# Finished sums of a feed-forward product stay in their PSUM banks instead of going to the stream one by one

## The chip, the cores and the metric

The kernel runs on one core of a Trainium2 chip. The metric is the device time of one execution in microseconds (us); lower is better. Runs of the kernel before: 1672.14, 1674.78 and 1675.12 us, median 1674.78.

## The reference

Two decoder layers over one sequence of 512 tokens with 1024 features, all float32:

```python
for l in range(DEPTH):                                   # DEPTH = 2
    x = x + 0.5 * swiglu(rms_norm(x, ffn1_norm[l]), ffn1_wg[l], ffn1_wu[l], ffn1_wd[l])
    h = rms_norm(x, mix_norm[l])
    z = h @ w_in[l]                                      # q | k | v | conv_B | conv_C | conv_h
    ...                                                  # windowed attention, short convolution
    x = x + jnp.concatenate([attn_out, conv_out], axis=-1) @ w_out[l]
    x = x + 0.5 * swiglu(rms_norm(x, ffn2_norm[l]), ffn2_wg[l], ffn2_wu[l], ffn2_wd[l])
return rms_norm(x, final_norm)

def swiglu(h, w_gate, w_up, w_down):                     # 1024 -> 2816 -> 1024
    return (jax.nn.silu(h @ w_gate) * (h @ w_up)) @ w_down
```

The change touches the last product of the four `swiglu` calls, `... @ w_down`, and its addition to `x`.

## The kernel before, in words

**Precision.** Every float32 operand is split in two: a high part `hi` (a cast on ScalarE, L205) and a remainder `lo = raw - hi` (a subtraction on VectorE, L206). A product is three TensorE passes: hi by hi, hi by lo, lo by hi. Weight pieces are 128x1024; their parts live in `wh` and `wl`, three buffers each, filled in the order written down by `plan` and taken by `take_split`, which keeps two pieces ahead. A buffer of `wh` is free again when TensorE has used the piece three before.

**The stream.** `x` stays in SBUF as eight tiles `xt(t, o)`, 128 tokens `t` by 512 features `o`.

**One feed-forward part** (`ffn`) goes through a list of stages: `p` and `u` make activations in blocks of 256 columns, `w` makes 512 columns with seven products in place of eight (`winograd2`), `s` is the down projection of four blocks at once with seven products (`share`), and `d` is the plain down projection of the blocks that are left (`down`, `down_end`, or `Finale` at the very end). The lists are

```python
FIRST = (("p", 0), ("p", 1), ("d", (0,)), ("w", 2), ("d", (1,)), ("w", 4), ("w", 6), ("w", 8), ("u", 10),
    ("s", 2), ("d", (10,)), ("s", 6))
INNER = (("p", 0), ("w", 1), ("d", (0,)), ("w", 3), ("w", 5), ("w", 7), ("w", 9), ("s", 1), ("s", 5),
    ("d", (9, 10)))
```

`FIRST` is used once, `INNER` twice, and `LAST`, which is `INNER` with `Finale` at its end, once. So each of the four parts has two groups of seven: s2 and s6 in `FIRST`, s1 and s5 in the others.

**A group of seven.** `share` runs the seven products, here called step 0 to step 6, into three pairs of banks: `x` (tag "mm", restarted at step 0 and carried on through steps 2, 4 and 6), `w` (tag "aux", step 1) and `y` (tag "sc", steps 3 and 5). Each step has two weight pieces, 2h0 and 2h1 being those of step 2; the text calls a piece's 12 matmuls a turn, so that a group is 14 turns. After the second piece of a step VectorE adds the bank pair to the tiles of the stream that `SHARES` names, one `scalar_tensor_tensor` of 128x512 for each bank (L910). The operands (`fb_s`, `ft_s`) are sums of activation blocks `raw_a`, made by `Seven.make` on VectorE (L672 to L678) and split. Step 2 needs a weight that is the sum of two pieces, made on VectorE in `need_split` (L233).

**Work from the block before.** The activations of a `w` stage come back through a DMA transpose; four copies on ScalarE join their halves (`join`, L1137, tile `raw_a<-pt`), and for block 9, which goes to `d`, two splits make the operands (`part`, tile `a`). `turns` runs these at fixed numbers of turns after the `w` stage.

**The end of a part.** `down_end` runs its 96 matmuls in an order of its own, takes its first weight in a tile `wx`, and adds each finished bank to the stream (L1213) before the next norm reads it. PSUM has eight banks: four "mm", two "sc", two "aux".

Order on each engine: TensorE, VectorE and ScalarE follow a scheduler's list order, not the source; only a few parts are fixed by hand (`by_hand`). Each engine then executes its list in order.

Of the kernel before, what the change touches and what calls it, by code (L numbers as in the profile page):

```python
# [16 lines left out]
P = 128  # L17
D = 1024
S = 512
# [6 lines left out]
NT = S // P  # L26
# [47 lines left out]
def trunk_kernel(  # L74
# [259 lines left out]
                        need_split(first + j + 3)  # L334
                        done(j, accs[j])

    def down(acts, blocks):

        last = len(blocks) - 1

        def products(acc, t, i, wh, wl):
            tok = slice(t * P, (t + 1) * P)
            ah, al = acts[blocks[i]]
            for k in range(2):
                for n, (a, w) in enumerate(((ah, wh), (al, wh), (ah, wl))):
                    nc.tensor.matmul(  # L346
                        acc,
                        a[:, k, tok],
                        w[:, k, :],
                        start=i + k + n == 0,  # L350
                        stop=i == last and k == 1 and n == 2,
                    )

        for o in range(2):
            accs = [psum("mm", [P, S], f"down_{state['group']}_{t}") for t in range(NT)]
            for i in range(last + 1):
                _, wh, wl = take_split()
                for t in range(NT):
                    products(accs[t], t, i, wh, wl)
                    if i == last:  # L360
                        yield t, o, accs[t]

    def down_end(acts, blocks, norm):

        a, b = blocks
        held = []

        def tile_of(n):
            while len(held) <= n:
                held.append(take_split(max(0, min(SPLIT_AHEAD, 3 - len(held))))[1:])  # L370
            return held[n]

        def products(acc, t, n):
            tok = slice(t * P, (t + 1) * P)
            ah, al = acts[blocks[n % 2]]
            wh, wl = tile_of(n)
            for k in range(2):
                for i, (x_, w) in enumerate(((ah, wh), (al, wh), (ah, wl))):
                    nc.tensor.matmul(  # L379
                        acc,  # L380
                        x_[:, k, tok],
                        w[:, k, :],
                        start=n % 2 + k + i == 0,
                        stop=n % 2 == 1 and k == 1 and i == 2,
                    )
# [12 lines left out]
        for o in range(2):  # L398
            accs = {t: bank(t, o) for t in (2, 3)}
            for i in range(2):  # L400
                n = 2 * o + i
                for t in (2, 3):
                    products(accs[t], t, n)
                    if i:
                        yield t, o, accs[t]
                if n in (1, 2):
                    norm.pull()
                if n:
                    need_split(ahead + n - 1)
# [473 lines left out]
            if norm:  # L883
                norm.pull()

    def share(ops, by, between=None, soon=None, after=None, each=lambda: None):


        accs = {}
        chains, shares = (CHAINS_EARLY, SHARES_EARLY) if after else (CHAINS, SHARES)  # L890
        for step, (acc, operand, start) in enumerate(chains):
            ops.make(operand)
            if after and step == 4:
                by_hand()
            xh, xl = ops.forms[operand]
            if start:
                tag = {"x": "mm", "y": "sc", "w": "aux", "z": "mm"}[acc]
                accs[acc] = [psum(tag, [P, S], f"{acc}_{ops.name}_{m}") for m in range(2)]
            for h in range(2):
                _, wh, wl = take_split()  # L900
                stream(accs[acc], wh, wl, xh, xl, h, start, after if step == 6 else None)
                each()
                if soon:
                    ops.make(*soon.get((step, h), ()))
                if h == 0:
                    continue
                for o, t, sign in shares[step]:
                    for m in range(2):
                        part = xt(2 * t + m, o)
                        nc.vector.scalar_tensor_tensor(  # L910
                            part, accs[acc][m], by * sign, part, op0=ALU.mult, op1=ALU.add
                        )
                        if after and (step, (o, t)) in ENDS_EARLY:
                            after(2 * t + m, o)
            if not soon and step < 3:
                ops.make(chains[step + 4][1])
            if between:
                between(step)

    def ahead(ops, at):  # L920
        return lambda step: ops.make(*at.get(step, ()))
# [2 lines left out]
    def ffn(norm, stages, whole, after=None, late=None):  # L924
# [137 lines left out]
        def winograd2(b, at, between=None):  # L1062
# [107 lines left out]
        raws = {}  # L1170
        pending = {}
        clock = [0]

        for i, (what, b) in enumerate(stages):
            final = i + 1 == len(stages)
            if final and after:
                after.begin()
            if what in "wu" and stages[i + 1][0] == "s":
                ops = shared(sevens[0])
                if what == "w":  # L1180
                    winograd2(b, i, ahead(ops, {3: ("b11",), 4: ("b21",), 5: ("t2",), 6: ("t3",)}))
                else:
                    winograd(b, ahead(ops, {1: ("b11",), 2: ("b21",), 4: ("t2",), 6: ("t3",)}))
            elif what == "w":
                winograd2(b, i)
            if what == "s" and b == sevens[0]:
                then = shared(sevens[1])
                sums = ("t3", "t2") if stages[-1] == ("s", sevens[1]) else ("t2", "t3")
                soon = ahead(then, {3: ("b11",), 4: ("b21",), 5: sums[:1], 6: sums[1:]})
                share(ops, 0.5, soon, each=turns)  # L1190
            elif what == "s":
                share(
                    then,
                    0.5,
                    each=turns,
                    after=after if final else None,
                )
            if what == "p":
                (plain if first else plain_halves)(b)
                if b == 0 and late:  # L1200
                    turn_rows(1)
            if what != "d":
                continue
            if final and not after:
                Finale().down(
                    [(acts[k][0][:, j, :], acts[k][1][:, j, :]) for k in b for j in range(2)]
                )
                return
            ends = down_end(acts, b, after) if final else down(acts, b)
# [12 lines left out]

    class Finale:

        def __init__(self):
# [14 lines left out]

        def products(self, rhs, half, t, c0, wide):

            acc = psum("mm", [P, wide], f"end_{half}_{t}_{c0}")
            tok = slice(t * P, (t + 1) * P)
            cols = slice(c0, c0 + wide)
            for k, (ah, al) in enumerate(rhs):
                wh, wl = self.w[half][k]
                nc.tensor.matmul(acc, ah[:, tok], wh[:, cols], start=k == 0, stop=False)  # L1250
                nc.tensor.matmul(acc, ah[:, tok], wl[:, cols], start=False, stop=False)
                nc.tensor.matmul(acc, al[:, tok], wh[:, cols], start=False, stop=k + 1 == len(rhs))
            return acc

        def close(self, acc, half, t, c0, ssq):
# [316 lines left out]
```

## Time and profile before

| | before |
|---|---|
| median of three runs | 1674.78 us |
| the profiled execution | 1674.87 us |
| its span, first to last instruction | 1673.1 us |
| TensorE busy | 1646.3 us, 7912 matmuls |
| VectorE busy | 1335.3 us, 1752 instructions |
| ScalarE busy | 1083.6 us, 1519 instructions |
| additions of banks to the stream, L910 `x_s`, `y_s`, `w_s` | 64 + 32 + 16 of 0.69 us |

The profile is one execution. A row of the timeline reads: start in us from the span's start, length in us, engine, line, operation, output<-inputs, shape, number of merged instructions, and in brackets how long the engine stood idle before it and what ended that. A row of the windows reads: the window, its length, then for each engine busy us and in brackets the number of instructions that touch the window, then the granted share of TensorE's clock, the DMA share and GB/s. PE is TensorE, DVE VectorE, ACT ScalarE.

### The profile page before, as it was taken

How to read it: one execution, taken by the hardware profiler on the slowest of the kernel's cores; microseconds unless marked ns; L12 is line 12 of the kernel's file. 1: busy time of each engine (PE TensorE's matmuls, PEld its weight loads, DVE VectorE, ACT ScalarE, POOL GpSimd, SP SyncE). 2: the span in 40 equal slices, each digit the busy share in tenths (PEclk: the TensorE clock that was granted, in tenths of full speed). 3: DMA queues.
4: the chain of work that ended last, by engine and by line, in shares of the span. 5: the costliest groups of instructions: out<-in, count | busy, mean ns of one | idle time of the engine just before them, and what ended most of it. 6: DMA issues, size and time to landing. Idle time of an engine off the chain costs nothing.

```text
span 1673.1 us, 21633 instructions
## 1 busy us (share of the span) xinstructions
PE 1646.3 (98%) x7912; PEld 1377.8 (82%) x7912; DVE 1335.3 (80%) x1752; ACT 1083.6 (65%) x1519; POOL 182.3 (11%) x164
## 2 busy tenths in 40 slices
PE   9999999999999999999999999999999999999998
PEld 7888897888888888887898888877988888888877
DVE  7977689967799777799687777996587987768995
ACT  6457776556566577785465777764565765777764
POOL 0011111000110111111001111110001101111111
PEclk9999999999999999999999999999999999999999
DMA  9369998821495788999636899985225946899981
GB/s 252 99 178 216 230 226 227 196 69 54 129 220 125 188 201 216 227 229 219 187 94 176 209 221 223 239 206 152 59 62 144 223 115 171 218 215 226 237 227 66
DMA packets 269568, 299.77 MB, mean 179 GB/s; under 512 B 89205, under 2 KB 153749, under 8 KB 269461
## 3 DMA queue, kind: packets, MB, share of 16 engines
q1 hardware_dynamic: 231156, 223.27, 45.4%
q0 software_dynamic: 37600, 74.46, 26.3%
q8 instruction: 62, 1.02, 0.2%
q10 hardware_dynamic: 704, 0.66, 0.1%
q14 instruction: 46, 0.37, 0.1%
HBM read 263.74 MB, written 2.10 MB: 159 GB/s over the span
## 4 chain that ended last, share of the span: by engine, by line
PE 81%; DVE 11%; DMA 4%; issue 2%; ACT 2%; SPq 1%; POOL 0%; ACTq 0%; DVEq 0%; POOLq 0%
PE x L875 24%; PE y L875 12%; PE w L875 6%; PE x_s L875 6%; DVE wl L206 4%; PE acc L296 4%; PE acc L297 4%; PE acc L299 4%; PE down L346 3%; PE y_s L875 3%; PE down L379 3%; PE acc L323 3%; PE x_m L875 2%; DMA raw<-in_ffn_wd_dram 2%; DVE x L910 1%
## 5 line engine op out<-in xcount | busy, mean ns | idle before, releaser
L206 DVE TENSOR_TENSOR wl<-raw,wh 128x1024 fp32r<-128x1024 f32 (+1 forms) x493 | 596.7, 1216 | 223.0 <-ACT wh L205 215.0
L205 ACT CAST wh<-raw 128x1024 fp32r<-128x1024 f32 (+1 forms) x493 | 513.6, 1044 | 396.3 <-PE y L875 61.5
L875 PE MATMUL x<-wh,fb 128*128 128x512 f32 x608 | 187.4, 389 | 0.1
L875 PE MATMUL y<-wh,ft 128*128 128x512 f32 x608 | 187.2, 389 | 0.0
L875 PE MATMUL x<-wh,ft 128*128 128x512 f32 x608 | 187.2, 389 | 0.0
L875 PEld LDWEIGHTS x<-wh,ft 128*128 128x128 f32 x608 | 114.1, 188 | 23.7
L875 PEld LDWEIGHTS y<-wh,ft 128*128 128x128 f32 x608 | 114.1, 188 | 23.7
L875 PEld LDWEIGHTS x<-wh,fb 128*128 128x128 f32 x608 | 113.9, 188 | 24.0 <-DVE x L1213 0.5
L875 PE MATMUL x<-wl,ft 128*128 128x512 f32 x304 | 118.3, 389 | 0.0
L875 PE MATMUL y<-wl,ft 128*128 128x512 f32 x304 | 118.3, 389 | 0.0
L875 PE MATMUL x<-wl,fb 128*128 128x512 f32 x304 | 118.3, 389 | 0.0
L1137 ACT COPY raw_a<-pt 128x1024 uint16<-128x1024 uint16 x76 | 103.1, 1356 | 17.8 <-DMA pt<-pl 17.7
L200 POOL DMA_DIRECT2D raw<-in_ffn_wu_dram x39 | 47.2, 1210 | 523.2 <-DMA raw<-in_ffn_wu_dram 399.8
L296 PE MATMUL acc<-hh,wh 128*128 128x512 f32 x240 | 94.6, 394 | 0.0
L299 PE MATMUL acc<-hh,wl 128*128 128x512 f32 x240 | 93.9, 391 | 0.0
L297 PE MATMUL acc<-hl,wh 128*128 128x512 f32 x240 | 93.6, 390 | 0.0
L875 PE MATMUL w<-wh,fb 128*128 128x512 f32 x304 | 93.6, 389 | 0.0
L875 PE MATMUL x_s<-wh,ft_s 128*128 128x512 f32 x256 | 80.3, 400 | 6.7 <-ACT wh L205 6.7
L875 PE MATMUL y_s<-wh,ft_s 128*128 128x512 f32 x256 | 78.9, 389 | 0.0
L200 POOL DMA_DIRECT2D raw<-in_ffn_wg_dram x39 | 47.1, 1220 | 275.5 <-DVE wl L206 109.2
L875 PE MATMUL x_s<-wh,fb_s 128*128 128x512 f32 x240 | 74.0, 389 | 0.0
L233 DVE TENSOR_TENSOR raw<-raw,raw 128x1024 f32<-128x1024 f32 x58 | 70.5, 1222 | 0.5
(326 smaller groups left out, 3478.6 us busy)
## 6 DMA issues: line engine op xcount, KB each, us to landing
raw<-in_ffn_wu_dram SPq DMA_DIRECT2D x126, 512.0 KB, 4.9
raw<-in_ffn_wd_dram SPq DMA_DIRECT2D x104, 512.0 KB, 5.8
raw<-in_ffn_wg_dram SPq DMA_DIRECT2D x86, 512.0 KB, 4.8
raw<-in_ffn_wu_dram POOLq DMA_DIRECT2D x39, 512.0 KB, 7.4
raw<-in_ffn_wg_dram POOLq DMA_DIRECT2D x39, 512.0 KB, 5.8
raw<-in_w_in_dram SPq DMA_DIRECT2D x36, 512.0 KB, 4.0
raw<-in_ffn_wd_dram POOLq DMA_DIRECT2D x32, 512.0 KB, 7.1
raw<-raw POOLq DMA_DIRECT2D x20, 512.0 KB, 7.2
```

Of the source, the lines that this page charges most:

```text
L200: nc.gpsimd.dma_start(out=r, in_=rows_of(*more), accum_op=ALU.add)
L205: cast = nc.scalar.copy(hi, raw)
L206: eng.tensor_sub(lo, raw, f32(hi))
L233: nc.vector.tensor_add(a11, a11, s1)
L296: nc.tensor.matmul(acc, hi[:, k, :], rhs[k][0], start=k == first, stop=False)
L297: nc.tensor.matmul(acc, hi[:, k, :], rhs[k][1], start=False, stop=False)
L299: nc.tensor.matmul(acc, lo[:, k, :], rhs[k][0], start=False, stop=k == last)
L323: nc.tensor.matmul(accs[j][:, t * H : (t + 1) * H], w[:, k, :], x_, start=t + k + i == 0, stop=k == KC - 1 and i == 2, skip_group_check=True,)
L346: nc.tensor.matmul(acc, a[:, k, tok], w[:, k, :], start=i + k + n == 0, stop=i == last and k == 1 and n == 2,)
L379: nc.tensor.matmul(acc, x_[:, k, tok], w[:, k, :], start=n % 2 + k + i == 0, stop=n % 2 == 1 and k == 1 and i == 2,)
L875: nc.tensor.matmul(accs[u], x_[:, 2 * h + k, tok], w[:, k, :], start=start and h + k + i == 0, stop=h + k == 2 and i == 2, skip_group_chec ...
L1137: nc.scalar.copy(room.rearrange("p c (n z) -> p c z n", z=2)[:, :, z, :], turned[0][:, NT * z + 2 * c : NT * z + 2 * c + 2, :],)
```

## The change

Three pairs of finished sums have a factor of +0.5 into one place of the stream: `w` into (t, o) = (0,0), `y` into the second half of the features, `x` at step 6 into the second half of the tokens. They are no longer added when they are finished:

- `w` keeps its two banks through both groups of seven: the second group accumulates onto it.
- Where a plain stage `d` follows a group, `y` after step 5 and `x` after step 6 stay open too, and `down`, `down_end` or `Finale.products` accumulate onto these banks instead of starting new ones; their own addition to the stream then carries both sums.
- In `FIRST`, `w` is passed on by `d` without an addition to the group s6.
- The turns of `join` and `part` are set anew: joins at 6 + 2·gap + gap·n turns in place of 8 + gap·n (with a gap of 2 that is 10, 12, 14, 16 in place of 8, 10, 12, 14), parts at 23 and 26 in place of 16 and 18.

The built program has 32 fewer VectorE instructions, eight in each part; the numbers of matmuls and of DMAs and their queues' order are the same. The order changes on TensorE, VectorE and ScalarE around the groups of seven only.

```diff
-    def down(acts, blocks):
+    def down(acts, blocks, open_):
...
-                        start=i + k + n == 0,
+                        start=i + k + n == 0 and fresh[t],
...
+            fresh = [(t, o) not in open_ for t in range(NT)]
+            accs = [
+                psum("mm", [P, S], f"down_{state['group']}_{t}") if fresh[t] else open_[t, o]
+                for t in range(NT)
+            ]
...
-    def down_end(acts, blocks, norm):
+    def down_end(acts, blocks, norm, open_):
...
         def bank(t, o):
+            if (t, o) in open_:
+                return open_[t, o]
             return psum("mm", [P, S], f"down_{state['group']}_{t}_{o}")
...
-    def share(ops, by, between=None, soon=None, after=None, each=lambda: None):
+    def share(
+        ops, by, between=None, soon=None, after=None, each=lambda: None, w=None, kept=()
+    ):
...
+            if acc == "w" and w:
+                accs[acc], start = w, False
...
-                if h == 0:
+                if h == 0 or step in kept:
                     continue
...
+    def going_on(accs):
+        where = {(0, 0): "w", (0, 1): "y", (1, 0): "x"}
+        return {(2 * t + m, o): accs[n][m] for (t, o), n in where.items() for m in range(2)}
...
-            plan += [(8 + gap * n, join, n) for n in range(4)]
+            plan += [(6 + 2 * gap + gap * n, join, n) for n in range(4)]
             if b not in blocks:
-                plan += [(16 + 2 * c, part, c) for c in range(2)]
+                plan += [(23 + 3 * c, part, c) for c in range(2)]
...
-                share(ops, 0.5, soon, each=turns)
+                goes_on = stages[i + 1][0] == "d"
+                accs = share(ops, 0.5, soon, each=turns, kept=(1, 5, 6) if goes_on else (1,))
+                w = accs["w"]
+                open_ = going_on(accs) if goes_on else {}
...
+                    w=w,
+                    kept=() if final else (1, 5, 6),
                 )
+                open_ = going_on(accs) if not final else {}
...
             for n, (t, o, acc) in enumerate(ends):
+                if w and not final and any(acc is z for z in w):
+                    continue
```

More of the change, by code (lines that the diff above doesn't have):

```diff
@@ L349, in products @@
                         w[:, k, :],
-                        start=i + k + n == 0,
+                        start=i + k + n == 0 and fresh[t],
                         stop=i == last and k == 1 and n == 2,
+                        skip_group_check=not fresh[t],
                     )
         for o in range(2):
-            accs = [psum("mm", [P, S], f"down_{state['group']}_{t}") for t in range(NT)]
+            fresh = [(t, o) not in open_ for t in range(NT)]
[3 more added lines that the diff above has]
+            ]
             for i in range(last + 1):
@@ L374, in products @@
             tok = slice(t * P, (t + 1) * P)
+            fresh = (t, n // 2) not in open_
             ah, al = acts[blocks[n % 2]]
@@ L382, in products @@
                         w[:, k, :],
-                        start=n % 2 + k + i == 0,
+                        start=n % 2 + k + i == 0 and fresh,
                         stop=n % 2 == 1 and k == 1 and i == 2,
+                        skip_group_check=not fresh,
                     )
         def bank(t, o):
+            if (t, o) in open_:
+                return open_[t, o]
             return psum("mm", [P, S], f"down_{state['group']}_{t}_{o}")
@@ L1172, in ffn @@
         clock = [0]
+        w, open_ = None, {}
         for i, (what, b) in enumerate(stages):
@@ L1204, in ffn @@
             if final and not after:
-                Finale().down(
+                Finale(open_).down(
                     [(acts[k][0][:, j, :], acts[k][1][:, j, :]) for k in b for j in range(2)]
@@ L1208, in ffn @@
                 return
-            ends = down_end(acts, b, after) if final else down(acts, b)
+            ends = down_end(acts, b, after, open_) if final else down(acts, b, open_)
             for n, (t, o, acc) in enumerate(ends):
+                if w and not final and any(acc is z for z in w):
+                    continue
                 if b == (0,) and first:
@@ L1223, in trunk_kernel, with __init__ @@
     class Finale:
-        def __init__(self):
+        def __init__(self, open_):
+            self.open = open_
             self.y = [[xt(t, half) for half in range(2)] for t in range(NT)]
@@ L1243, in products @@
         def products(self, rhs, half, t, c0, wide):
-            acc = psum("mm", [P, wide], f"end_{half}_{t}_{c0}")
+            fresh = (t, half) not in self.open
+            acc = psum("mm", [P, wide], f"end_{half}_{t}_{c0}") if fresh else self.open[t, half]
             tok = slice(t * P, (t + 1) * P)
@@ L1249, in products @@
                 wh, wl = self.w[half][k]
-                nc.tensor.matmul(acc, ah[:, tok], wh[:, cols], start=k == 0, stop=False)
-                nc.tensor.matmul(acc, ah[:, tok], wl[:, cols], start=False, stop=False)
-                nc.tensor.matmul(acc, al[:, tok], wh[:, cols], start=False, stop=k + 1 == len(rhs))
+                last = k + 1 == len(rhs)
+                for n, (a, w) in enumerate(((ah, wh), (ah, wl), (al, wh))):
+                    nc.tensor.matmul(
+                        acc,
+                        a[:, tok],
+                        w[:, cols],
+                        start=k + n == 0 and fresh,
+                        stop=last and n == 2,
+                        skip_group_check=not fresh,
+                    )
             return acc
```

3 lines of the change are left out of this document (2 added, 1 removed).

## The prediction

> **What bounds the kernel now.** I read the page's totals first, then who TensorE waited for, then the windows.
>
> ```profile
> span 1673.1 us, 21633 instructions
> PE 1646.3 (98%) x7912; PEld 1377.8 (82%) x7912; DVE 1335.3 (80%) x1752; ACT 1083.6 (65%) x1519; POOL 182.3 (11%) x164
> ```
>
> TensorE is busy for all but 26.8 us of the span, and the change removes no matmul. So the most that any edit of this kind can bring is what TensorE loses in stops, and the question is where these are.
>
> ```profile
> PE x_s L875 <- ACT wh L205: 6.7, 4, 1.9
> PE down L379 <- ACT wx L205: 3.0, 2, 2.5
> PE x_s L875 <- DVE wl L206: 2.9, 7, 0.5
> ```
>
> In this list of TensorE's waits the three longest belong to the groups of seven (`x_s`) and to the plain down projection behind them. How much time is lost there, the windows say; their columns are length, then busy us and instruction count for PE, PEld, DVE, ACT and POOL.
>
> ```profile
> 250.00:275.00 25.00, 23.42 (x103) 18.59 (x101) 24.42 (x27) 20.27 (x22) 4.17 (x4) 1.00 0.84 212
> 700.00:725.00 25.00, 25.00 (x112) 20.71 (x111) 22.07 (x22) 21.05 (x25) 2.41 (x2) 1.00 0.88 220
> 750.00:775.00 25.00, 24.49 (x106) 19.56 (x106) 21.87 (x25) 16.39 (x17) 2.42 (x2) 1.00 1.00 260
> 775.00:800.00 25.00, 22.44 (x90) 17.30 (x90) 24.91 (x26) 13.44 (x14) 4.17 (x4) 0.93 0.82 193
> 1075.00:1100.00 25.00, 24.74 (x109) 20.19 (x108) 21.60 (x23) 16.43 (x16) 2.42 (x2) 1.00 0.98 243
> 1100.00:1125.00 25.00, 22.18 (x95) 17.34 (x94) 25.00 (x27) 15.91 (x16) 4.20 (x4) 1.00 0.86 181
> 1125.00:1150.00 25.00, 22.47 (x93) 18.02 (x92) 18.51 (x21) 9.51 (x10) 0.00 (x0) 0.93 0.76 229
> 1600.00:1625.00 25.00, 22.14 (x96) 17.36 (x95) 25.00 (x26) 15.89 (x16) 4.17 (x4) 1.00 0.88 180
> ```
>
> An undisturbed window (700 to 725) holds 112 matmuls of 512 columns, 0.223 us each. The six windows around the groups s1 and s5 of the three later feed-forward parts lack 6, 22, 3, 17, 19 and 16, together 83, which is 18.5 us. The window of `FIRST` lacks 9, 2.0 us. In the worst windows VectorE is busy 24.4 to 25.0 of 25 us: there it is the engine that is late, not TensorE.
>
> **Part by part: the stop before step 2 of the second group.** The timeline of the second part shows how it comes about; the two later parts have the same list.
>
> ```profile
> 751.85 1.05 ACT L205 CAST wh<-raw 128x1024 fp32r<-128x1024 f32 x1 [0.46 <-PE y_s L875]
> 757.24 1.36 ACT L1137 COPY raw_a<-pt 128x1024 uint16<-128x1024 uint16 x1 [4.34 <-DMA pt<-pl]
> 758.46 1.99 ACT L205 CAST wh<-raw 128x1024 fp32r<-128x1024 f32 x2
> 755.81 0.69 DVE L910 SCALAR_TENSOR_TENSOR x<-y_s,x 128x512 f32<-128x512 f32 x1
> 759.53 1.23 DVE L206 TENSOR_TENSOR wl<-raw,wh 128x1024 fp32r<-128x1024 f32 x1 [3.04 <-ACT wh L205]
> 760.04 0.61 PE L875 MATMUL y_s<-wh,ft_s 128*128 128x512 f32 x2
> 779.14 1.22 DVE L206 TENSOR_TENSOR a<-raw_a,a 128x1024 fp32r<-128x1024 f32 x1
> 780.28 1.29 DVE L910 SCALAR_TENSOR_TENSOR x<-x_s,x 128x512 f32<-128x512 f32 x2
> 781.47 1.22 DVE L206 TENSOR_TENSOR ft_s<-raw_a,ft_s 128x1024 fp32r<-128x1024 f32 x1
> 782.61 2.36 DVE L233 TENSOR_TENSOR raw<-raw,raw 128x1024 f32<-128x1024 f32 x2
> 784.88 0.69 DVE L910 SCALAR_TENSOR_TENSOR x<-w_s,x 128x512 f32<-128x512 f32 x1
> 785.48 2.36 DVE L206 TENSOR_TENSOR wl<-raw,wh 128x1024 fp32r<-128x1024 f32 x2
> 783.92 2.21 ACT L205 CAST wh<-raw 128x1024 fp32r<-128x1024 f32 x2 [4.68 <-DVE raw L233]
> 781.62 0.62 PE L875 MATMUL w_s<-wh,fb_s 128*128 128x512 f32 x2
> 782.30 0.62 PE L875 MATMUL w_s<-wh,fb_s 128*128 128x512 f32 x2
> 785.02 1.57 PE L875 MATMUL x_s<-wh,ft_s 128*128 128x512 f32 x4 [1.88 <-ACT wh L205]
> 788.20 1.01 PE L875 MATMUL x_s<-wl,ft_s 128*128 128x512 f32 x2
> ```
>
> ScalarE stands 4.34 us at the first join, whose transpose has not landed, and behind it in its queue stand the casts of two weight pieces that could have run. VectorE therefore idles 3.04 us and then works without a pause until the weight sum of step 2 (L233) at 782.61. Its cast starts at 783.92, and TensorE stands 1.88 us.
>
> What the change does to this. (1) The first join goes two turns later, behind those two casts. Three matmuls take 0.68 us (781.62 to 782.30), a turn of 12 takes 2.72. The cast at 751.85 started when TensorE freed a buffer; the next is freed one turn later, at 754.57, so it ends at 755.6, and VectorE goes on at 756.50 (755.81 + 0.69) in place of 759.53: 3.0 us gained. (2) The first `part` split leaves this stretch for the turns after it: 1.14 us gained (779.14 to 780.28). (3) The pair of `w` additions of s1 falls before the 3.04 us idle, and brings nothing here. From 759.53 to 782.61 are 23.1 us; without the split 21.9, so the sum would start at 778.4. Two pairs of additions must wait for TensorE's own step ends, which I estimate at 0.7 us of idle: 779.1. The sum's first half ends at 780.25, its cast at 781.35. TensorE comes to step 2 eight turns after 760.04, at 781.8. The stop of 1.88 us goes.
>
> What is late next. In the new list VectorE makes both halves of the sum, then another operand sum (L678, 1.14 us), and only then the first `wl`: 779.1 + 2.27 + 1.14 + 1.14 = 783.65. TensorE runs four products (0.91 us) to 782.7 and then meets two products of step 3 that the scheduler has pulled forward (`y_s` on piece 3h0). These need a third cast. ScalarE does it after the second half's, 781.45 to 782.5, so from 782.5 to 783.55. Everything on TensorE is queued behind this pair. TensorE stands 0.85 us, with the restart about 1.0 us. The bounds: the buffer for 3h0 is free only when step 1 ends, 781.8 + 1.05, so never under 0.2 us; if VectorE gains only the split, 3.1 us (worked out with the rivals). I take 1.0, since the idle it rests on is a row (3.04). For three parts: 3.0 us stay.
>
> **The pulled-forward `down` product.**
>
> ```profile
> 1131.92 1.04 ACT L205 CAST wx<-raw 128x1024 fp32r<-128x1024 f32 x1 [4.19 <-DMA raw<-in_ffn_wd_dram]
> 1133.02 0.50 PE L379 MATMUL down<-wx,a 128*128 128x512 f32 x1 [2.53 <-ACT wx L205]
> 1134.28 1.05 PE L875 MATMUL x_s<-wl,ft_s 128*128 128x512 f32 x2
> 1616.01 1.20 PE L875 MATMUL x_s<-wh,ft_s 128*128 128x512 f32 x4 [1.89 <-ACT wh L205]
> ```
>
> Because the operand `a` is ready early, one product of `down` stands in the middle of step 4, and TensorE waits 2.53 us for its weight. With the parts at turns 23 and 26, this product stands behind the whole of s5, and ScalarE casts `wx` behind three more weight pieces and the second part. The wait goes. What covers `wx` then: its load landed at 1131.9, when TensorE stood in the first piece of step 4, six turns or 16 us before `down`; the part has gained some 3 us up to there and the wait itself is 2.5, so about 10 us remain. After the stops of 1.88 and 2.53 us TensorE ran at half pace for a while (788.20 and 1134.28: 1.01 and 1.05 us for two products that take 0.62 at 781.62), and the windows' granted clock is 0.93. The stop of 1.89 us at 1616 had no such stretch: its four products took 1.20 us, those at 785.02 took 1.57. The 83 missing matmuls contain this loss.
>
> The Trainium skill, "TensorE: Matmul & The Clock Gate", Part 1, says that the clock falls to half only after an idle window of some 3.4 us. No stop here is that long, so by that rule the half pace would have another cause and stay; the rival below has its price.
>
> **`FIRST`.**
>
> ```profile
> 259.83 2.36 DVE L233 TENSOR_TENSOR raw<-raw,raw 128x1024 f32<-128x1024 f32 x2
> 262.70 1.22 DVE L206 TENSOR_TENSOR wl<-raw,wh 128x1024 fp32r<-128x1024 f32 x1
> 263.97 0.51 PE L875 MATMUL x_s<-wl,ft_s 128*128 128x512 f32 x1 [0.51 <-DVE wl L206]
> ```
>
> Here the stop is in the first group, and VectorE's list is unchanged up to L233, so it stays. After it L678 takes the place of one addition: `wl` starts at 259.83 + 2.27 + 1.14 = 263.2 in place of 262.70. That costs 0.5 us (bounds 0 and 1.1).
>
> **The other additions.** Of 32 removed, 0.69 us each or 22 us of VectorE, nearly all lie where TensorE does not wait (steps 5 and 6, the `w` pairs behind L233): nothing on the path. If the cover goes, that is, VectorE is late there too, each is worth at most its 0.69. The splits moved to turns 23 and 26 go into the same stretch, where these additions have left more room than they take. No DMA is moved past another on any queue.
>
> **Sum**, against the profiled execution of 1674.87 us (span 1673.1, the rest around it; the median of the runs shown is 1674.78, so no correction): 1674.9 - 18.5 + 3.0 + 0.5 = 1659.9, say **1660 us**.
>
> **Rivals.**
> - *VectorE stays late.* If the idle of 3.04 us is not won, the sum starts at 782.61 - 1.14 = 781.47 and its cast ends at 783.7, 1.9 us after TensorE comes; the third cast ends at 785.8, when TensorE has waited for it since 784.6: 3.1 us in place of 1.0. And the half pace (some 1.5 us) may follow in one of the three parts, half likely: 1660 + 6.3 + 0.8 = 1667. For it: the windows with 25.0 busy. Against: the queue's order on ScalarE.
> - *The half pace stays:* from 785.02 to the end of the row at 788.20 are 4.2 us, at double time at most 2.1 us of loss; I take 1.5 in each of two parts: 1663. Against: it followed only stops.
> - *A bank wait.* Eight banks are now held through the end of each part; if TensorE must wait at one place in each of four parts for a pair of additions (1.29 us), it is 1665. The next norm reads the stream after these same additions, so a waiter is hard to name. The Trainium skill, "PSUM — Partial Sum Buffer", Summary: rules for kernel authors, says to evacuate promptly because the space is tight, which speaks against held sums; no wait for a bank is among the long ones above.
> - *Transfers bind.* The DMA share of 0.82 at 90 matmuls becomes 1.02 at 112. If that is the limit, the stretches keep their length: 1674. Against: 750 to 775 has 1.00 with 106.
> - *Slower: `wx` late at `down`.* It is now cast behind everything, and `down` begins with it in two parts. If its load slips, TensorE has nothing else. It decides from a slip of 8 us (the 10 us above less cast and split); at 18 us each of two parts would stand 10 us and lose 1.5 to the half pace: 1660 + 23 = 1683. The 4.19 us above show that this load is not early.
>
> That the change does not do what it says is excluded by the built program: 32 fewer additions, and the lists quoted.
>
> **How the numbers follow.** Forecast 0.65, VectorE late 0.17, half pace 0.04, bank wait 0.03, transfers 0.04, `wx` 0.07. A measurement of this kernel can tell 0.2% (3.3 us) from no change, so the first four are faster: 0.89; transfers are the same: 0.04; slower 0.07. The range goes from the lower bound of the stops (3 x 0.8 and 0.5 less: 1657, and runs lie up to 2.6 us under the median) 1655.5, to the first rival, 1668.
>
> **What would show it.** In the new profile: no wait of TensorE for `wx` inside s5, no 4 us wait of ScalarE at the first join, windows around the groups with 108 or more matmuls and clock 1.00, a stop of about 1 us before `y_s` (not `x_s`) in step 2 of s5, and the stop in `FIRST` as long as before. A stop of 2 us or more there, or at `down`, would make it wrong.

## The result, and the profile after

The changed kernel takes 1658.25 us (median of four runs, 1657.86 to 1658.74); the kernel before took 1674.95 us beside it (four runs, 1672.14 to 1675.22). The ratio is 0.9904, with a 95% interval of 0.9887 to 0.9921. The forecast was 1660.0 us, range 1655.5 to 1668.0. The profiled execution took 1658.03 us, with a span of 1656.3.

The page of the changed kernel (line numbers have moved: L875 is now L884, L910 is L923, L1137 is L1155, L672 to L678 are L681 to L687): span, busy times, and the group of the joins with ScalarE's idle time ahead of them (4.9 us, where it was 17.8).

```profile
span 1656.3 us, 21592 instructions
PE 1641.2 (99%) x7912; PEld 1377.6 (83%) x7912; DVE 1317.0 (80%) x1720; ACT 1084.7 (65%) x1519; POOL 182.3 (11%) x164
L1155 ACT COPY raw_a<-pt 128x1024 uint16<-128x1024 uint16 x76 | 103.4, 1360 | 4.9 <-DMA pt<-pl 4.9
```

VectorE is busy 18.3 us less (1335.3 to 1317.0) and the span is 16.8 us shorter (1673.1 to 1656.3). These two numbers lie so close together that a second explanation suggests itself: the removed additions are the gain. The experiments put this against the forecast's explanation.

Who TensorE waited for, in the changed kernel: us in total, times, longest.

```profile
PE x_s L884 <- DVE wl L206: 1.1, 1, 1.1
...
PE y_s L884 <- ACT wh L205: 0.7, 3, 0.2
PE x_s L884 <- ACT wh L205: 0.7, 1, 0.7
```

The 6.7 us of `x_s` behind `wh` are 0.7, the 3.0 us of `down` behind `wx` are gone from the list, and a small new wait of `y_s` has come, 0.25 us in each of three places. A second profile of the same kernel ("the change again" below) has 0.25, 0.78 and 0.25 us there. The windows of the changed kernel:

```profile
250.00:275.00 25.00, 23.29 (x104) 18.65 (x103) 24.77 (x27) 18.23 (x20) 4.17 (x4) 1.00 0.88 218
750.00:775.00 25.00, 25.00 (x112) 20.71 (x111) 24.90 (x27) 16.75 (x17) 3.74 (x4) 1.00 1.05 277
775.00:800.00 25.00, 24.75 (x109) 20.17 (x109) 24.03 (x26) 14.33 (x14) 2.84 (x3) 1.00 0.89 229
1075.00:1100.00 25.00, 25.00 (x112) 20.71 (x111) 24.90 (x28) 17.47 (x17) 3.62 (x3) 1.00 1.08 263
1100.00:1125.00 25.00, 24.75 (x110) 20.17 (x109) 24.23 (x25) 14.41 (x14) 2.96 (x3) 1.00 0.90 218
1125.00:1150.00 25.00, 25.00 (x112) 20.70 (x111) 13.06 (x17) 11.74 (x18) 0.00 (x0) 1.00 0.61 173
1600.00:1625.00 25.00, 24.75 (x110) 20.17 (x109) 22.54 (x23) 15.30 (x16) 0.25 (x1) 1.00 0.61 166
```

The six windows of the three later parts lack 0, 3, 0, 2, 0 and 2 matmuls of 112, together 7, where they lacked 83. The difference of 76 times 0.223 us is 16.9 us: these places account for the whole shortening of the span. VectorE is now full a window earlier, 24.9 of 25 us in 750 to 775 and in 1075 to 1100, where it had 21.9 and 21.6; in the windows where it was late it now has 24.0, 24.2 and 22.5, where it had 24.9, 25.0 and 25.0.

The timeline of the changed kernel in the second part:

```profile
754.84 1.06 ACT L205 CAST wh<-raw 128x1024 fp32r<-128x1024 f32 x1 [1.67 <-PE y_s L884]
757.56 1.06 ACT L205 CAST wh<-raw 128x1024 fp32r<-128x1024 f32 x1 [1.66 <-PE x_s L884]
758.52 1.35 ACT L1155 COPY raw_a<-pt 128x1024 uint16<-128x1024 uint16 x1
756.69 1.22 DVE L206 TENSOR_TENSOR wl<-raw,wh 128x1024 fp32r<-128x1024 f32 x1
778.87 2.35 DVE L233 TENSOR_TENSOR raw<-raw,raw 128x1024 f32<-128x1024 f32 x2
781.14 1.21 DVE L687 TENSOR_TENSOR sums_s<-sums_s,raw_a 128x1024 f32<-128x1024 f32 x1
782.28 2.35 DVE L206 TENSOR_TENSOR wl<-raw,wh 128x1024 fp32r<-128x1024 f32 x2
780.20 3.14 ACT L205 CAST wh<-raw 128x1024 fp32r<-128x1024 f32 x3 [3.09 <-DVE raw L233]
782.07 1.07 PE L884 MATMUL x_s<-wh,ft_s 128*128 128x512 f32 x4
783.39 0.73 PE L884 MATMUL y_s<-wh,ft_s 128*128 128x512 f32 x2 [0.25 <-ACT wh L205]
```

The first join stands behind the casts of 754.84 and 757.56 and starts without a wait; `wl` starts at 756.69; step 2 starts at 782.07 with no stop ahead of it, where TensorE stood 1.88 us.

### The profile page after: what moved, and what is told of

The parts are those of the page before. It is cut to its first block, busy times and chain, and to the rows that moved or that the text cites. A ratio compares the mean times of both kernels' runs of the same rounds, so it can differ in the third digit from the quotient of the medians.

```text
span 1656.3 us, 21592 instructions
## 1 busy us (share of the span) xinstructions
PE 1641.2 (99%) x7912; PEld 1377.6 (83%) x7912; DVE 1317.0 (80%) x1720; ACT 1084.7 (65%) x1519; POOL 182.3 (11%) x164
## 4 chain that ended last, share of the span: by engine, by line
PE 92%; DVE 6%; ACT 1%; issue 1%; DMA 0%; POOL 0%; DVEq 0%; ACTq 0%; POOLq 0%
PE x L884 25%; PE y L884 12%; PE x_s L884 10%; PE w L884 6%; PE y_s L884 5%; PE acc L296 4%; PE acc L297 4%; PE acc L299 4%; PE down L346 3%; PE acc L323 3%; PE w_s L884 2%; DVE wl L206 2%; PE x_m L884 2%; PE up L1009 1%; PE acc L782 1%; DVE x L923 1%
## 5 line engine op out<-in xcount | busy, mean ns | idle before, releaser
L884 PE MATMUL x<-wh,fb 128*128 128x512 f32 x608 | 187.4, 389 | 0.1
L884 PE MATMUL x<-wh,ft 128*128 128x512 f32 x608 | 187.2, 389 | 0.0
L884 PE MATMUL y<-wh,ft 128*128 128x512 f32 x608 | 187.2, 389 | 0.0
L884 PEld LDWEIGHTS x<-wh,ft 128*128 128x128 f32 x608 | 114.1, 188 | 23.7
L884 PEld LDWEIGHTS y<-wh,ft 128*128 128x128 f32 x608 | 114.1, 188 | 23.7
L884 PEld LDWEIGHTS x<-wh,fb 128*128 128x128 f32 x608 | 113.9, 188 | 23.9 <-DVE x L1240 0.5
L884 PE MATMUL x<-wl,fb 128*128 128x512 f32 x304 | 118.3, 389 | 0.0
L884 PE MATMUL x<-wl,ft 128*128 128x512 f32 x304 | 118.3, 389 | 0.0
L884 PE MATMUL y<-wl,ft 128*128 128x512 f32 x304 | 118.3, 389 | 0.0
L1155 ACT COPY raw_a<-pt 128x1024 uint16<-128x1024 uint16 x76 | 103.4, 1360 | 4.9 <-DMA pt<-pl 4.9
L884 PE MATMUL w<-wh,fb 128*128 128x512 f32 x304 | 93.6, 389 | 0.0
L884 PE MATMUL y_s<-wh,ft_s 128*128 128x512 f32 x256 | 79.2, 390 | 0.7 <-ACT wh L205 0.7
L884 PE MATMUL x_s<-wh,ft_s 128*128 128x512 f32 x256 | 78.3, 390 | 0.7 <-ACT wh L205 0.7
L884 PE MATMUL x_s<-wh,fb_s 128*128 128x512 f32 x240 | 73.9, 389 | 0.0
L233 DVE TENSOR_TENSOR raw<-raw,raw 128x1024 f32<-128x1024 f32 x58 | 70.4, 1219 | 0.5
```

The costliest lines, as they stand in the source:

```text
L233: nc.vector.tensor_add(a11, a11, s1)
L884: nc.tensor.matmul(accs[u], x_[:, 2 * h + k, tok], w[:, k, :], start=start and h + k + i == 0, stop=h + k == 2 and i == 2, skip_group_chec ...
L1155: nc.scalar.copy(room.rearrange("p c (n z) -> p c z n", z=2)[:, :, z, :], turned[0][:, NT * z + 2 * c : NT * z + 2 * c + 2, :],)
```

## The experiments

T1 is the forecast's theory: the gain comes from the order of ScalarE's and VectorE's work ahead of step 2 of s5, which the two new lines of turns change. T2 is the rival: the gain is the 32 removed additions. The kernels were run in three groups of four, each on one chip together with the kernel before. That kernel's median was 1678.33 us beside the first four, 1679.83 beside the next four and 1679.49 beside the last four, so comparisons are made within a group, by ratio.

| kernel | median (lowest to highest), us | ratio to before, 95% interval |
|---|---|---|
| turns only | 1658.52 (1657.58 to 1659.59) | 0.9887 (0.9873 to 0.9901) |
| sums only | 1678.99 (1675.16 to 1681.15) | 1.0005 (0.9995 to 1.0015) |
| join turns only | 1667.27 (1666.62 to 1669.40) | 0.9941 (0.9928 to 0.9954) |
| part turns only | 1668.82 (1664.54 to 1670.80) | 0.9945 (0.9931 to 0.9960) |
| change, only `w` kept | 1661.10 (1659.15 to 1663.38) | 0.9891 (0.9871 to 0.9911) |
| change, only `y` and `x` kept | 1658.54 (1658.00 to 1659.60) | 0.9876 (0.9858 to 0.9895) |
| change, t4 asked for later | 1659.38 (1658.71 to 1662.15) | 0.9884 (0.9864 to 0.9903) |
| the same, step 0's additions later | 1657.16 (1656.29 to 1658.78) | 0.9869 (0.9850 to 0.9887) |
| turns, step 0's additions later | 1656.23 (1654.72 to 1658.09) | 0.9864 (0.9842 to 0.9887) |
| the change again | 1660.71 (1658.82 to 1661.61) | 0.9891 (0.9871 to 0.9910) |
| turns only again | 1657.99 (1656.70 to 1660.13) | 0.9877 (0.9857 to 0.9896) |
| t4 and step 0's additions later, again | 1656.45 (1654.79 to 1657.38) | 0.9866 (0.9844 to 0.9888) |

### The turns without the sums

```diff
 # the kernel before
-            plan += [(8 + gap * n, join, n) for n in range(4)]
+            plan += [(6 + 2 * gap + gap * n, join, n) for n in range(4)]
...
-                plan += [(16 + 2 * c, part, c) for c in range(2)]
+                plan += [(23 + 3 * c, part, c) for c in range(2)]
```

> The kernel before with the two new lines of turns (first join two turns later, parts of the later split later) and none of the kept sums: all 32 additions of the sums are made as before. T1 (the order of ScalarE's and VectorE's work ahead of step 2 of stage s5 makes the gain): nearly all of it comes, 1660 us (1658.5 to 1663); no join waits 4 us for its transposing transfer, no down product with wx stands ahead of step 2, the three later stretches lose 1 to 2 us each where they lost 5.9, 8.6 and 3.7; the first part keeps its 2.2 us. T2 (the gain is the 32 removed additions, some 18 us of VectorE): 1673 to 1675, VectorE busy 1335 and the stops as before.

Measured: 1658.52 us, the whole gain, with every addition still made. The page of this kernel, and its timeline at step 2 of s5 in the second part:

```profile
PE 1640.7 (99%) x7912; PEld 1378.7 (83%) x7912; DVE 1333.6 (81%) x1752; ACT 1083.7 (65%) x1519; POOL 182.5 (11%) x164
```

```profile
779.28 2.36 DVE L233 TENSOR_TENSOR raw<-raw,raw 128x1024 f32<-128x1024 f32 x2
781.55 0.69 DVE L910 SCALAR_TENSOR_TENSOR x<-w_s,x 128x512 f32<-128x512 f32 x1
782.15 2.35 DVE L206 TENSOR_TENSOR wl<-raw,wh 128x1024 fp32r<-128x1024 f32 x2
782.48 1.07 PE L875 MATMUL x_s<-wh,ft_s 128*128 128x512 f32 x4
783.43 0.50 PE L875 MATMUL x_s<-wl,ft_s 128*128 128x512 f32 x1
```

VectorE is busy 1333.6 us here, 16.6 more than in the changed kernel, and the span is 1656.1 us, 0.2 shorter. T2 is out. The rows also show what the addition of `w` did where it stood: 0.69 us at 781.55, after which `wl` starts at 782.15. In the changed kernel that place is free, and the sum for t4 (L687, 1.21 us) stands in it: `wl` starts at 782.28, although L233 came 0.41 us earlier. Here the scheduler has no product of step 3 ahead of `x_s<-wl`, and there is no stop for `y_s`. The six windows of the three later parts lack 5 matmuls together, where 1 to 2 us in each part had been expected.

### The sums without the turns

```diff
 # the changed kernel
-            plan += [(6 + 2 * gap + gap * n, join, n) for n in range(4)]
+            plan += [(8 + gap * n, join, n) for n in range(4)]
...
-                plan += [(23 + 3 * c, part, c) for c in range(2)]
+                plan += [(16 + 2 * c, part, c) for c in range(2)]
```

> The changed kernel with the old turns of joins and parts; all sums stay in their banks. T1: the stop before step 2 of s5 stays in the three later parts (1 to 2 us each, and slow products behind it), and so does the 4 us wait of the first join. The down product with wx that was pulled ahead of step 2 no longer is, as the kept banks order the down products otherwise, so its 3 us and some of the slow products go: 1667 us (1664 to 1671). T2: the whole gain, 1657 to 1660.

Measured: no change, ratio 1.0005. Its page and waits:

```profile
PE 1648.7 (98%) x7912; PEld 1379.9 (82%) x7912; DVE 1315.7 (79%) x1720; ACT 1083.6 (65%) x1519; POOL 182.3 (11%) x164
...
L1155 ACT COPY raw_a<-pt 128x1024 uint16<-128x1024 uint16 x76 | 103.3, 1359 | 19.1 <-DMA pt<-pl 19.1
```

```profile
PE x_s L884 <- ACT wh L205: 6.7, 4, 1.9
PE x_s L884 <- DVE wl L206: 4.6, 6, 1.1
```

VectorE has lost 19.6 us of work against the kernel before (1335.3 to 1315.7), and none of it is in the time. My 1667 was wrong as well. The pulled-forward product and its wait for `wx` did go, as I had said, but something came in its place. The timeline of this kernel at step 2 of s5, second part:

```profile
782.85 2.35 DVE L233 TENSOR_TENSOR raw<-raw,raw 128x1024 f32<-128x1024 f32 x2
785.12 1.22 DVE L687 TENSOR_TENSOR sums_s<-sums_s,raw_a 128x1024 f32<-128x1024 f32 x1
786.26 1.22 DVE L206 TENSOR_TENSOR wl<-raw,wh 128x1024 fp32r<-128x1024 f32 x1
785.25 1.19 PE L884 MATMUL x_s<-wh,ft_s 128*128 128x512 f32 x4 [1.89 <-ACT wh L205]
787.53 0.50 PE L884 MATMUL x_s<-wl,ft_s 128*128 128x512 f32 x1 [1.08 <-DVE wl L206]
```

The stop of 1.89 us is unchanged, and a second one of 1.08 us follows, because the free place has been taken by L687 and `wl` starts at 786.26 instead of 785.48. In the third and fourth parts TensorE also ran at half pace behind it (below). So the ratio of 1.0005 is a balance: the wait for `wx` (3.0 us) went, the waits of `x_s` for `wl` grew from 2.9 to 4.6 us, and the clock was at half for 10.2 us in place of 6.8. A shorter list for VectorE was not an earlier `wl`.

### Each line of turns alone

> The kernel before with the new line of join turns alone. T1: the casts that stood behind the join's wait come earlier, VectorE gains 3.0 us in s1 and the stop of 1.88 us before step 2 of s5 shrinks to 0.5 to 1.2; the pulled-forward down product and its wait for wx stay (3.0 us): 1665 us (1661 to 1669). T2: 1673 to 1675.

> The kernel before with the new line of part turns alone. T1: the split of the first part (1.14 us of VectorE) leaves the stretch, the stop before step 2 goes from 1.88 to about 0.8 us, and the down product with wx is no longer ahead of step 2 (its waits of 2.53 and 0.51 us go, with the slow products behind): 1665 us (1662 to 1669); the join keeps its wait of 4 us. The last part has no parts to move and keeps its stop. T2: 1673 to 1675.

Measured: ratios 0.9941 and 0.9945, that is 0.59% and 0.55%; the two lines together give 1.13%, so the shares add up within their intervals. With the join alone (first ScalarE's row of its first join, TensorE's of step 2, second part, and the product in the third):

```profile
759.85 1.35 ACT L1137 COPY raw_a<-pt 128x1024 uint16<-128x1024 uint16 x1
783.76 1.19 PE L875 MATMUL x_s<-wh,ft_s 128*128 128x512 f32 x4 [0.21 <-ACT wh L205]
1128.51 0.80 PE L379 MATMUL down<-wx,a 128*128 128x512 f32 x1 [2.71 <-ACT wx L205]
```

The join no longer waits and the stop is 0.21 us, but the product of `down` still waits 2.71 us for its weight, with half pace behind it (the window's clock is 0.86). With the parts alone:

```profile
759.31 1.36 ACT L1137 COPY raw_a<-pt 128x1024 uint16<-128x1024 uint16 x1 [4.02 <-DMA pt<-pl]
785.98 1.20 PE L875 MATMUL x_s<-wh,ft_s 128*128 128x512 f32 x4 [0.77 <-ACT wh L205]
```

The product of `down` has left the group (no wait for `wx` remains), the stop is 1.1 us shorter, which is the split's 1.14, and the join waits 4.02 us as before. The last part was expected to have no split to move and to keep its stop. That was wrong: in the kernel before, a split stands in its list at 1610.14 too, and with the parts alone its stop is 0.77 us where it was 1.89.

At the stop before step 2 the two lines overlap: one takes 1.67 of the 1.88 us, the other 1.11. What each leaves alone lies elsewhere as well: with the join, the waits for `wx` (3.9 us in two places) and the half pace; with the parts, the rest of the stops of `x_s` (3.4 us for `wh`, 3.2 for `wl`). That the shares add up so well is therefore no proof that the losses are separate.

### Which sum in its bank costs the stop before `y_s`

```diff
 # the changed kernel, w alone kept
-        where = {(0, 0): "w", (0, 1): "y", (1, 0): "x"}
+        where = {(0, 0): "w"}
...
-                accs = share(ops, 0.5, soon, each=turns, kept=(1, 5, 6) if goes_on else (1,))
+                accs = share(ops, 0.5, soon, each=turns, kept=(1,))
...
-                    kept=() if final else (1, 5, 6),
+                    kept=() if final else (1,),
```

The other kernel keeps `y` and `x` in the same way (`kept=(5, 6)`) and adds `w` to the stream after step 1, as before.

> The changed kernel with w alone kept; y and x are added to the stream and started again as before, 16 additions more than the changed kernel. The removed additions pay nothing on TensorE's path by T1, so this is the changed kernel's time, 1658.3 us (1657 to 1660); if the place of w's addition, now free for the 1.21 us sum of t4 ahead of wl in step 2, is what makes the stop of 0.53 us in the three later parts, that stop is here too, and about 1.05 us in the first. If the removed additions paid by themselves (T2), half of their gain would be missing: 1666.

> The changed kernel with y and x kept and w added as before. T1: the changed kernel's time, 1658.3 us (1656.5 to 1660); w's addition of 0.69 us stands ahead of wl in step 2 of s5 again and the sum of t4 behind it, so the stop of 0.53 us of the later parts goes, as with the turns alone. T2: 1666.

Measured: 1661.10 and 1658.54 us, ratios 0.9891 and 0.9876, whose intervals overlap; neither is near T2's 1666. The traces tell them apart where the times do not. With `w` kept, the second part has L687 at 784.23 ahead of `wl`, and the stop before `y_s` is there in all three parts (0.7 us in total). With `w` added, its addition stands ahead of `wl` again, and the list of waits has none of `y_s`:

```profile
783.83 0.68 DVE L923 SCALAR_TENSOR_TENSOR x<-w_s,x 128x512 f32<-128x512 f32 x1
784.43 2.35 DVE L206 TENSOR_TENSOR wl<-raw,wh 128x1024 fp32r<-128x1024 f32 x2
```

So the new small stop belongs to `w` kept in its bank, through the place that it frees.

### t4 later, and step 0's additions later

The first kernel asks for the sum of t4 after step 2 in place of step 1:

```diff
-            if not soon and step < 3:
-                ops.make(chains[step + 4][1])
+            if not soon and step in (0, 2):
+                ops.make(*(chains[n][1] for n in ((4,) if step == 0 else (5, 6))))
```

> The changed kernel with the sum and split of t4 made after step 2 instead of after step 1 of each group of seven. T1: nothing but casts' own work stands between L233 and wl of step 2, wl is 1.1 us earlier, and the stop of 1.05 us in the first part goes, with the 0.53 us of each later part: 1656 us (1655 to 1657.5). Rival (those stops are set by ScalarE's casts, not by VectorE's order, or come back at step 5, which takes t4): 1658 to 1660.

Measured: 1659.38 us, no gain, and the edit did not reach what it was aimed at. Its second part:

```profile
782.48 1.22 DVE L687 TENSOR_TENSOR sums_s<-sums_s,raw_a 128x1024 f32<-128x1024 f32 x1
783.61 3.49 DVE L206 TENSOR_TENSOR wl<-raw,wh 128x1024 fp32r<-128x1024 f32 x3
```

L687 is still ahead of `wl`: VectorE's order is the scheduler's, and it filled the place again. So this run does not test whether an earlier `wl` ends the stop. The second kernel besides makes the additions of step 0 after the first half of step 1:

```diff
-                if h == 0 or step in kept:
+                first = not after and (step, h) == (1, 0)
+                if not first and (h == 0 or step in kept or step == 0 and not after):
                     continue
-                for o, t, sign in shares[step]:
+                done, sums = (0, accs["x"]) if first else (step, accs[acc])
+                for o, t, sign in shares[done]:
...
-                            part, accs[acc][m], by * sign, part, op0=ALU.mult, op1=ALU.add
+                            part, sums[m], by * sign, part, op0=ALU.mult, op1=ALU.add
```

> As the kernel with t4 made later, and besides the additions of step 0 (x, two of 0.64 us) are made after the first half of step 1 instead of ahead of it, in the three plain kinds of groups. T1: L233 comes up to 1.28 us earlier, and the first part's stop of 0.65 us for wh goes too: 1655 us (1654 to 1657). Rival (L233 waits for its transfers or for the split ahead of it, or the additions stand ahead of wl instead): no better than with t4 later alone, 1656 to 1659.

Measured: 1657.16 us. The runs of the two kernels overlap by 0.07 us (1658.78 and 1658.71), so this pair alone does not settle the gain. The weight's first half is made ahead of the additions and cast early, `wl` no longer waits for the second half, and the waits of `y_s` are gone (this kernel, second part):

```profile
777.90 1.22 DVE L233 TENSOR_TENSOR raw<-raw,raw 128x1024 f32<-128x1024 f32 x1
779.23 1.05 ACT L205 CAST wh<-raw 128x1024 fp32r<-128x1024 f32 x1 [0.76 <-DVE raw L233]
780.78 1.22 DVE L206 TENSOR_TENSOR wl<-raw,wh 128x1024 fp32r<-128x1024 f32 x1
```

### Four kernels on one chip: with and without the sums

The changed kernel, the turns alone, and each of them with step 0's additions later (with the sums it is the kernel just shown, with t4 asked for later).

> The turns alone (no kept sums), and the additions of step 0 made after the first half of step 1 in the three plain kinds of groups. T1: as good as the same with the kept sums, within 1 us of it, and within 1 us of the turns alone in the later parts, which have 0.15 us left to gain each; 1657.5 us. If the kept sums help by leaving VectorE 18 us more room, it is 1 to 3 us slower than the kernel that has them.

> The changed kernel itself on the same chip as the other three, to compare them directly: 1658.3 us; the turns alone within 1 us of it by T1, 16 us slower by T2.

> The turns alone on the same chip as the changed kernel. T1: within 1 us of it (1657.5 to 1659.5). If the kept sums add a gain of their own that two chips had hidden, 1 to 3 us slower.

> The changed kernel with t4 asked for later and the additions of step 0 later, on the same chip as the changed kernel: 1 us faster than it (1656.5 to 1658), since its three later parts have no stop of 0.53 us left; rival (the stops that went come back elsewhere): within 0.3 us of it.

Measured: with step 0's additions later, 1656.23 us without the sums and 1656.45 with them: the sums make no difference that these runs can tell. The changed kernel took 1660.71 us, and both of these lie below it with no overlap of the runs (1654.72 to 1658.09 and 1654.79 to 1657.38 against 1658.82 to 1661.61). The turns alone took 1657.99 (1656.70 to 1660.13), which overlaps with the changed kernel; if the sums cost it something, the stop before `y_s` in three parts (1.3 us in this profile) accounts for half of the 2.7, and the rest isn't explained. The gain of the kernel with both later was 4.3 us, where about 1 had been expected. In its profile the stops before `y_s` are gone (1.3 us) and those in `FIRST` are 0.20 us where the changed kernel has 1.71; the rest is not explained. Its window of the worst place:

```profile
775.00:800.00 25.00, 25.00 (x112) 20.72 (x111) 23.96 (x25) 13.17 (x14) 1.78 (x3) 1.00 0.92 239
```

112 matmuls: TensorE does not stop there any more. The best versions found beat the changed kernel by some 0.25%, and one of them needs no held sum.

## Why the prediction was right

- **The bound.** TensorE's stops around the groups of seven. Of the 83 missing matmuls 76 came back. But TensorE's idle 26.8 us were not the most to be had, as I read them: of the 16.8 us, 11.7 came out of its idle time and 5.1 out of its busy time (1646.3 to 1641.2), which held the products at half pace.
- **Step 1, the join.** The cast was forecast for 754.57 and came at 754.84; VectorE was to go on at 756.50 and did at 756.69. The join alone is worth 0.59%.
- **Step 2, the split.** Its 1.14 us came out as 1.1 (the stop of 1.88 us is 0.77 with the parts alone).
- **The start of the sum and step 2.** L233 was forecast for 779.1 and came at 778.87; step 2 for 781.8, with no stop, and came at 782.07. The 0.7 us of idle in that sum did not come: VectorE's list has no gap above 0.05 us between 756.69 and 778.87, its instructions only took 0.24 us more. The start, 0.19 us late, made up for part of that.
- **The stop that was to stay.** The place (`y_s`, pulled forward) and the releaser (a third cast) were right, and the size was not: 0.85 us and a restart were forecast, 0.25 us came. ScalarE's three casts took 3.14 us from 780.20, so the third ended at 783.34 and not 783.55; and TensorE, which started step 2 0.27 us later than I had it and whose four products ended 1.07 us after their start, where I had counted 0.91, came to the pair at 783.14, not 782.7. The 3.0 us for three parts are 7 missing matmuls, 1.6 us. The size is not a fixed one: in the second profile one of the three stops is 0.78 us, near the 0.85.
- **The product of `down`.** No wait for `wx` remains; the cover held: ScalarE casts `wx` without a wait at 803.5 and 1130.4, 6.3 and 12.8 us before the first product that uses it. But I gave its going to the parts alone. The sums alone also remove it, since the kept banks give `down` another order.
- **`FIRST`.** Forecast 0.5 us longer. The stop changed its halves: before step 2 it is 0.65 us where the kernel before had 1.08, then 1.05 behind `wl` where it had 0.51, together 0.1 more; the window holds 104 matmuls where it held 103. L687 does stand ahead of `wl`, as forecast, but I had not seen that the first half would shrink.
- **The other additions: nothing on the path.** The clearest evidence is the pair with the new turns and step 0's additions later: 1656.23 us without the sums and 1656.45 with them. The 1.0005 of the sums alone is a balance of gains and losses. The 22 us of VectorE came out as 18.3. What I missed is that the place of an addition does not stay empty: I had L678 moving up ahead of `wl` without asking whether the addition it replaces was the cheaper of the two (0.69 against 1.21 us).
- **The rivals.** Transfers do not bind: the DMA share is 1.05 and 1.08 in windows with 112 matmuls. No wait for a bank is in the list of the first profile; the second has one of 0.48 us at 114.63, ahead of all held sums, where the kernel before has 0.16. So the advice in the Trainium skill, "PSUM — Partial Sum Buffer", Summary: rules for kernel authors, to evacuate promptly, has no price in this trace. The half pace went with the stops, so the rival by which it stays is out; the clock is 1.00 in all windows shown of the changed kernel.
- **The range.** Its lower end, 1655.5, is not what its terms give: 1657 less 2.6 is 1654.4. None of the changed kernel's runs lies between the two.

## What to carry to other kernels

Ask of removed work on a busy engine what will stand in its place: here 18 us less on an engine that was 25.0 of 25 us busy at the critical place bought no time that the runs can tell. Most of the removed work stood where nothing waited for it, and at the one place ahead of a waiting consumer a longer operation moved up into the gap. Moving two kinds of operations that were not needed yet bought everything. A change with two ideas in it should be run as two. And when a saving of busy time and a saving of span agree to 10%, that is no evidence that one is the other.

## What the runs showed of the hardware

Half pace follows short stops, but not always. The turns alone were run twice. In the first profile the stop of 1.05 us in `FIRST` is followed by pairs that take 1.05 us in place of 0.62, until the granted clock rises again at 266.66:

```profile
261.30 1.21 PE L875 MATMUL x_s<-wh,ft_s 128*128 128x512 f32 x4 [1.05 <-ACT wh L205]
263.01 0.61 PE L875 MATMUL x_s<-wl,ft_s 128*128 128x512 f32 x1 [0.50 <-DVE wl L206]
263.42 1.06 PE L875 MATMUL x_s<-wh,ft_s 128*128 128x512 f32 x2
```

In the second profile of the same program the stop is 1.03 us at the same place, and the products behind it run at full pace. Over the kernels here, one of eight stops of 1.03 to 1.08 us ahead of step 2 in `FIRST` was followed by half pace, three of six of 1.88 to 1.89 us (once only behind a second stop of 1.07 us), and both of 2.53 and 2.71. The traces also record each change of the granted clock: between the start and the last matmuls they have four stretches at half clock of 3.41 us and two of 6.83.

This record shows what tells the cases apart. In every profile the changes of the granted clock lie whole multiples of 3.41 us apart. In the kernel before it falls at 785.64, rises at 789.05, falls at 1133.80, rises at 1137.21 and falls at 1669.69, behind the last matmul: 1, 101, 1 and 156 such steps. If each trace is cut into windows of 3.41 us along these steps, the two profiles of the turns alone differ in where the cut falls (the first two rows are from the first profile, the others from the second):

```profile
259.84:263.25 3.41, 1.86 (x7) 0.91 (x6) 3.41 (x5) 3.05 (x3) 1.76 (x2) 1.00 0.66 125
263.25:266.66 3.41, 3.41 (x9) 2.64 (x9) 3.41 (x4) 2.81 (x4) 0.00 (x0) 0.50 1.04 193
260.53:263.94 3.41, 2.38 (x10) 1.35 (x8) 3.41 (x4) 2.26 (x3) 1.58 (x2) 1.00 0.73 135
263.94:267.35 3.41, 2.89 (x14) 2.36 (x13) 3.41 (x5) 3.41 (x5) 0.18 (x1) 1.00 1.12 213
```

In the first, both stops (1.05 and 0.50 us) fall into one window, TensorE is idle for 1.55 of its 3.41 us, and the clock of the next window is 0.50. In the second, the cut separates them (1.03 and 0.52 us), and the clock stays at 1.00. Over all fourteen profiles, between the start and the last matmuls, a window at full clock with 1.55, 1.88, 1.89, 1.93, 2.01 and 2.53 us of idle time was followed by half clock, one with 1.72 was not, and none of the 24 windows with 1.0 to 1.5 was. This is read from the traces; no run moves a stop against the steps to test it.

The Trainium skill, "TensorE: Matmul & The Clock Gate", Part 1, gives an idle window of about 3.4 us for the fall to half clock, and calls this window free-running. The trace agrees with both the length of the window and its not starting with the stop; that TensorE must be idle for all of it does not hold here, where 1.55 us were enough once and 1.88 us and more each time.

The half pace explains only a part of the scatter. The kernel before spread over 5.7 us in 17 executions on one chip, with granted clocks of 0.994 to 0.999, and its slower executions have the lower clocks in the main. But the sums alone, which spread over 6.0 us in 12, took 1678.20 us at a clock of 0.997 and 1675.77 at 0.995, and the parts alone spread over 6.3 us in six with the clock at 0.997 to 1.000. The turns alone spread over 2.0 us in four executions and 3.4 in five. What makes the rest of the scatter is open.
